# The last expert pair in four column groups, and two vectors on another DMA queue

## The chip, the cores and the metric

The kernel runs on one core of one Trainium2 chip. The metric is the device time of one execution in microseconds; each kernel is executed several times and the median counts. One execution per kernel is recorded by the hardware profiler, and the rows below come from that one. Five engines work side by side, each through its own list in order: TensorE (PE, matmuls; its weight loads are shown as PEld), VectorE (DVE), ScalarE (ACT), GpSimd (POOL) and SyncE (SP), which here mostly issues transfers. A "q" behind an engine's name (SPq, ACTq) is its queue of issued transfers.

## The reference, cut to what matters

One layer of an encoder on 512 tokens of 1024 columns. First a token mixer and a layer norm, then a mixture of experts and a second layer norm. The change touches only the end, the experts and the second norm:

```python
def expert_block(args):
    xs, e = args
    return (jax.nn.silu(xs @ w1[e]) * (xs @ w3[e])) @ w2[e]
...
y = yb.reshape(-1, d) * row_w[:, None].astype(x.dtype)
return jax.ops.segment_sum(y, rows, num_segments=t + 1)[:t]
...
moe = _hier_moe(x.reshape(-1, D_MODEL), ...)
x = _layer_norm(DEEPNORM_ALPHA * x + moe, ln2_g[layer], ln2_b[layer])
```

There are 32 experts with w1 and w3 of 1024 x 512 and w2 of 512 x 1024 in fp32, 2 MB each. Every token goes to two of them.

## The kernel before, in words

**Experts in pairs.** Experts are taken in 16 pairs `q` (0 to 15, `NP` is 16), 64 token places for each expert of a pair (`u` is 0 or 1). `gemm1` (line 1001) makes the first products with w1 (`m` = 0) and w3 (`m` = 1): the two experts of a pair use the two halves of PE's columns. `h` is their product after silu, `turn` (line 1016) transposes it to `hT`, and `gemm2` (line 1024) makes the second product with w2 into PSUM tiles `y`, one of 128 x 512 for columns 0 to 511 and one for 512 to 1023. `weigh` (line 1039) writes `y` times the token's weight as two addends of fewer bits: ACT writes `yh`, and DVE writes `yl`, the rest of `y` that `yh` leaves. `part` (line 1052) is the combine: PE multiplies the selection matrix `sel` with `yh` and `yl` of some columns, for a block `j` of 128 tokens, into a PSUM tile `cb`, and DVE adds that to the sum `xa`. For pairs 0 to 14 `combine` (line 1057) does this for the pair before, spread over the work of the present one.

**Weights.** `load_next` (line 664) issues the next of 96 loads on SP's queue, each of 2 MB, into nine slots of SBUF that are reused in turn. `queued` (line 115) keeps the transfers of one engine in the order of the program. A load waits until the products that read its slot's former content are done. The loads for w2 of the last pair are four halves of 1 MB (lines 686 to 691), the first two for columns 0 to 511, the others for the rest. When pair 14's w3 product is in the program, all 96 are issued.

**Order.** `kp` (line 98) pins an instruction behind the one before it in the program on the same engine, a transfer issued by an engine among them. An instruction on PE, DVE and ACT below runs in the order in which it is written, with one exception: the copy `onrow` (line 1165) is not pinned, and DVE's order starts anew there.

**Second norm's vectors.** At pair 14 (`q == NP - 2`, line 1110), behind `gemm1(q, 1)`, two transfers bring `ln2_g` and `ln2_b`, each copied to all 128 partitions (512 KB each), into `lnv`, the slot that this very product has read last. Before, they are issued on SP behind all weights. ACT's next instructions there in the program are the two copies of `xg` in `turn_rows` (line 905) and the copy of `hT`. At the end of pair 15 (lines 1120 to 1122) ACT copies `ln2_b` of one row to `off[0]` and DVE makes `off[1]`, the rest. `offset` (line 1169) multiplies them with a row of ones on PE, as the start of the last output's PSUM tiles `fp`.

**The last pair's second product.** It is cut by columns, `CS` (line 1143), in three groups: 512, 256 and 256. In program order: product and weighing of group 0; product and weighing of group 1; `add` of group 0 for all four token blocks; `squares` of the first 512 columns of blocks 0 and 1; `add` of group 1 for blocks 0 and 1; product and weighing of group 2; `squares` for blocks 2 and 3; `add` of group 1 for blocks 2 and 3; then for each block `add` of group 2 and `squares` of the second half. `add` (line 1148) is `part` on PE and, on DVE, the addition to `xa` that also sums the row into `sm2`; for group 0 a small DVE step `k2` follows. `squares` (line 1158) is on ACT and sums the squares of 512 columns around `k2`.

**The end.** From line 1225 on DVE makes means and variances, POOL a power, `newton` an iteration of it, ACT the diagonal matrices `dg`. The output of five of the eight tiles of 128 x 512 (`TURN`) goes through PE, with `dg` as weights (`scaled`), and ACT; DVE makes the other three (`finish`).

Of the kernel before, what the change touches and what calls it, by code (L numbers as in the profile page):

```python
# [10 lines left out]
F32 = mybir.dt.float32  # L11
# [6 lines left out]
ALU = mybir.AluOpType  # L18
# [4 lines left out]
D = 1024  # L23
K8 = 8
NT = 4
# [5 lines left out]
NP = NE // 2  # L31
# [38 lines left out]
def bcast_rows(ap2, n):  # L70

    return bass.AP(tensor=ap2.tensor, offset=ap2.offset, ap=[[0, 128], [1, n]])
# [7 lines left out]
def body(ctx, tc, nc, a):  # L80
    L, R = "left", "right"

    def pool(stack, name, side, **kw):
        return stack.enter_context(tc.tile_pool(name=name, bufs=1, side=side, reuse_waits="tile", **kw))
# [10 lines left out]
    def mm_tile(name="mm", tag="mm", shape=(128, 512)):  # L95
        return ps.tile(list(shape), F32, name=name, tag=tag, bufs=2 if tag == "lv" else 3)

    def kp(op):

        def pinned(*x, **y):  # L100
            ins = op(*x, **y)  # L101
            e = ins.ins.engine
            prev = next((i for i in reversed(nc.cur_bb.bb.instructions)
                         if i is not ins.ins and i.engine == e and type(i).__name__ != "BassTilePoolBoundary"), None)
            if prev is not None:
                edge(ins, prev.name)
            return ins
        return pinned

    def edge(ins, name):  # L110
        tc.add_manual_dep(ins.ins, name, mybir.DependencyInfo(mybir.DependencyClass.NoSync, mybir.DependencyReason.DATA), reason="order")
# [3 lines left out]
    def queued(op):  # L115

        def issue(*x, **y):
            ins = op(*x, **y)
            e = str(ins.ins.engine)
            if e in tail:  # L120
                edge(ins, tail[e])
            tail[e] = ins.ins.name
            return ins
        return issue
# [749 lines left out]
    def onehot_next(q):  # L874
        oq[q] = ep.tile([128, NT, 128], BF, name="oq", bufs=2)
        onehot(q, oq[q])
# [82 lines left out]
    ep = pool(ctx, "ep", R)  # L959
# [3 lines left out]
    j = NT - 1  # L963
# [21 lines left out]
    def first_fetch():  # L985

        yield
        p = slots(1, lambda j: ti[:, j, :], 2)
        tok1 = ep.tile([128, 1], F32, name="tok1")
        kp(nc.vector.tensor_reduce)(tok1, p[:, 0:2], axis=AX.X, op=ALU.add)  # L990
        pre["rows"] = fetch(tok1)
        run(share())
        yield
# [30 lines left out]
    def gemm2(q, st, cs=((0, 512), (512, 512)), last=True):  # L1024
        raw = [held[2, q, u] for u in range(2)]
        for c, d in cs:
            n, s = c // 512, slice(c % 512, c % 512 + d)
            if c % 512 == 0:
                st["y"][n] = mm_tile("y", "am")
            for f in range(4):  # L1030
                for u in range(2):
                    kp(nc.tensor.matmul)(st["y"][n][u * CAP:(u + 1) * CAP, s], st["hT"][:, f, u * CAP:(u + 1) * CAP],
                                         raw[u][:, f, c:c + d], start=(f == 0), stop=(f == 3))
        if last:
            for u in range(2):
                held.pop((2, q, u))
                load_next()

    def weigh(st, cs=((0, 512), (512, 512))):
        if "yh" not in st:  # L1040
            yy = mo.tile([128, 2, D], F32R, name="yy", tag="ln")
            st["yh"], st["yl"] = yy[:, 0], yy[:, 1]
            st["sel"] = ep.tile([128, T], F32R, name="sel")
            kp(nc.vector.tensor_scalar)(st["sel"], i512, -float(NOTOK), st["tw"][:, 0:1], op0=ALU.add, op1=ALU.is_equal)
        w = st["tw"][:, 1:2]
        for c, d in cs:
            s = slice(c, c + d)
            y = st["y"][c // 512][:, c % 512:c % 512 + d]
            kp(nc.scalar.activation)(st["yh"][:, s], y, AF.Copy, scale=w)
            kp(nc.vector.scalar_tensor_tensor)(st["yl"][:, s], y, w, st["yh"][:, s].bitcast(F32), op0=ALU.mult, op1=ALU.subtract)  # L1050
# [6 lines left out]
    def combine(st, first=False):  # L1057
        for i in range(8):
            j, c = divmod(i, 2)
            s = slice(c * 512, c * 512 + 512)  # L1060
            p = mm_tile("cb", ("mm", "am")[i % 2])
            part(p, st, j, c * 512, 512)
            if first:
                kp(nc.vector.scalar_tensor_tensor)(xa[:, j, s], xa[:, j, s], ALPHA, p, op0=ALU.mult, op1=ALU.add)
            else:
                kp(nc.vector.tensor_add)(xa[:, j, s], xa[:, j, s], p)
            yield
# [24 lines left out]
    for q in range(NP):  # L1092
        st = prs.setdefault(q, {"y": {}})
        old, last, back = prs.get(q - 1), q == NP - 1, iter(())
        if last:

            with tc.If(nov > 0):
                overflow(tc, nc, a, dram, x1d, xa, rc, ident, nblk, oh_, rk_, w_, nov, mm_tile, wp, *[slot[(len(order) - i) % len(HOME)] for i in (7, 8)])
            back = combine(old)
        p = gemm1(q, 0, first_fetch() if q == 0 else iter(()))  # L1100
        ac = wp.tile([128, FE], F32, name="ac", tag="btmp", bufs=2)
        kp(nc.scalar.activation)(ac, p, AF.Silu)
        if old and not last:
            gemm2(q - 1, old)
            weigh(old)
            back = combine(old, q == 1)
        if q > NP - 3:
            run(islice(back, 4 if last else 3))
        p = gemm1(q, 1)
        if q == NP - 2:  # L1110
            lnv = slot[(len(order) - 9) % len(HOME)].rearrange("p (i d) -> p i d", i=4)
            for i, x in enumerate((a["ln2_g"], a["ln2_b"])):
                queued(nc.sync.dma_start)(lnv[:, i], bcast_rows(x, D))
        h = wp.tile([128, FE], F32, name="h", tag="wraw", bufs=4)
        kp(nc.vector.tensor_mul)(h, ac, p)
        if last:
            run(islice(back, 3))
            st["hT"] = turn(h)
            run(back)
            off = [ep.tile([128, D], F32R, name="off", tag=t) for t in ("rows", "xg")]  # L1120
            kp(nc.scalar.copy)(off[0][0:1], lnv[0:1, 1])
            kp(nc.vector.tensor_sub)(off[1][0:1], lnv[0:1, 1], off[0][0:1].bitcast(F32))
            break
        xg = turn_rows(pre.pop("rows") if q == 0 else rows)
        for n in range(0 if q == 0 else q + 2, min(q + 3, NP)):
            prs.setdefault(n, {"y": {}})["tw"] = weights(n)
        if q < NP - 2:
            rows = fetch(prs[q + 2]["tw"][:, 0:1])
        if q < NP - 3:
            onehot_next(q + 3)  # L1130
        run(islice(back, 8 if q < NP - 2 else 3))
        st["hT"] = turn(h)
        run(back)
        if q == NP - 2:
            gemm2(q, st)
            weigh(st)
        if q == 1:
            run(cnt)
        if q == 3:
            nov = nc.values_load(novi[0:1, 0:1], min_val=0, max_val=NOV)  # L1140
        prs.pop(q - 1, None)

    CS = ((0, 512), (512, 256), (768, 256))
    sm2 = ep.tile([128, NT, 3], F32, name="n2s")
    sq2 = ep.tile([128, NT, 2], F32, name="n2q")
    k2, d2 = [ep.tile([128, NT], F32, name=n) for n in ("n2k", "n2d")]

    def add(j, i, tag):

        c, d = CS[i]  # L1150
        p = mm_tile("cb", tag)[:, 0:d]
        s = slice(c, c + d)
        part(p, st, j, c, d)
        kp(nc.vector.scalar_tensor_tensor)(xa[:, j, s], xa[:, j, s], 1.0, p, op0=ALU.mult, op1=ALU.add, accum_out=sm2[:, j, i:i + 1])
        if i == 0:
            kp(nc.vector.tensor_scalar)(k2[:, j:j + 1], sm2[:, j, 0:1], -1.0 / 512, None, op0=ALU.mult)

    def squares(j, n):

        junk = wp.tile([128, FE], F32, name="sq", tag="btmp", bufs=2)  # L1160
        kp(nc.scalar.activation)(junk, xa[:, j, hs[n]], AF.Square, bias=k2[:, j:j + 1], accum_out=sq2[:, j, n:n + 1])
# [10 lines left out]
        for i in range(2):  # L1172
            kp(nc.tensor.matmul)(pf[x], onrow, off[i][0:1, hs[x[1]]], start=(i == 0), stop=False)

    gemm2(NP - 1, st, [CS[0]], False)
    weigh(st, [CS[0]])
    gemm2(NP - 1, st, [CS[1]], False)
    weigh(st, [CS[1]])
    for j in range(NT):
        add(j, 0, ("mm", "lv")[j % 2])  # L1180
    squares(0, 0)
    squares(1, 0)
    add(0, 1, "mm")
    add(1, 1, "am")
    gemm2(NP - 1, st, [CS[2]])
    weigh(st, [CS[2]])
    squares(2, 0)
    squares(3, 0)
    add(2, 1, "lv")
    add(3, 1, "lv")  # L1190
    for j in range(NT):
        add(j, 2, ("mm", "lv")[j % 2])
        squares(j, 1)
    for i, x in enumerate(TURN):
        offset(x, "mm" if i < 3 else "am")
# [223 lines left out]
```

## Time and profile before

| | us |
|---|---|
| median of 3 runs | 1281.15 |
| lowest and highest | 1279.73 and 1282.1 |
| the profiled execution, its own time | 1280.67 |
| span of its records | 1278.0 |
| PE busy in the span | 1235.9 (97%) |
| DVE busy | 669.9 (52%) |
| ACT busy | 360.7 (28%) |
| mean rate of transfers | 224 GB/s |

Busy shares are means over a long row of stages with different limits: PE 97% doesn't say that PE limits the stage in question. Matmuls are pipelined and their ends are modelled, and some matmul records can be missing. The view of busy time by stretch tells for each stretch how busy each engine was, the granted clock of PE (1.00 is 2.4 GHz, 0.50 is 1.2 GHz), and the share of the 16 transfer engines in use. In the timeline a bracket tells how long the engine had been idle before a row and what released it; rows of the same kind that follow each other are merged (x and a count). A line number of 101 is that of `kp`, so most rows here have it; they are told apart by the tile names, out<-in.

### The profile page before, as it was taken

To read this page: it belongs to the slowest core of one execution; us is meant where nothing else is said; L and a number is where in the kernel's file an instruction comes from. 1 tells how busy PE (TensorE), PEld (TensorE's weight loads), DVE (VectorE), ACT (ScalarE), POOL (GpSimd) and SP (SyncE) were. 2 spreads that over 40 slices of the span, in tenths; PEclk is the share of its full clock that TensorE was granted. 3 is DMA by queue.
4 is the path that set the end of the run, shared out by engine and by line. 5 is a ranking of instruction groups with operands and counts; after the bars stand their busy time and mean duration, and the time that the engine had idled before them with its cause. 6 is when DMAs were issued, how large, how long until landed. Compare 5 with 4: busy or idle time off the path is not lost.

```text
span 1278.0 us, 20529 instructions
## 1 busy us (share of the span) xinstructions
PE 1235.9 (97%) x8369; PEld 851.2 (67%) x8369; DVE 669.9 (52%) x1412; ACT 360.7 (28%) x704; POOL 105.3 (8%) x117
## 2 busy tenths in 40 slices
PE   7999999999999999999999999999999999889997
PEld 7887877878778878888888798344444443333444
DVE  4587878877882246556555467332432222222326
ACT  4443444443452223222333231111111111111114
POOL 0031222302100000000000001100100000000000
PEclk9999999999999999999999999999999999999998
DMA  6322223222233333232335498999999999999992
GB/s 211 95 72 69 74 66 85 76 78 73 75 90 124 124 97 91 73 100 81 91 108 160 148 346 340 365 426 429 427 427 428 426 426 428 428 427 428 428 409 104
DMA packets 94000, 286.02 MB, mean 224 GB/s; under 512 B 13531, under 2 KB 71163, under 8 KB 81616
## 3 DMA queue, kind: packets, MB, share of 16 engines
q1 hardware_dynamic: 84112, 267.80, 54.6%
q10 hardware_dynamic: 7056, 10.78, 3.1%
q0 software_dynamic: 2736, 6.12, 1.2%
q8 instruction: 66, 1.08, 0.4%
q14 instruction: 30, 0.25, 0.1%
HBM read 282.19 MB, written 6.32 MB: 226 GB/s over the span
## 4 chain that ended last, share of the span: by engine, by line
PE 78%; DMA 15%; DVE 4%; ACT 1%; issue 1%; SPq 0%; POOL 0%; ACTq 0%; DVEq 0%; POOLq 0%
PE mm L237 13%; PE g L101 13%; DMA raw<-in_w_dram 12%; PE mm L239 12%; PE mm L238 12%; PE y L101 5%; PE op L101 3%; PE cb L101 3%; PE vp L252 2%; PE vp L253 1%; PE vp L254 1%; PE lv L386 1%; PE tr L101 1%; PE lv L421 1%; PE vp L101 1%; DMA raw<-in_ln_b_dram 1%
## 5 line engine op out<-in xcount | busy, mean ns | idle before, releaser
L101 PE MATMUL g<-raw,xg 128*64 128x512 f32 x1024 | 240.1, 602 | 15.4 <-DMA raw<-in_w_dram 15.0
L237 PE MATMUL mm<-xT,w 128*128 128x512 f32 x576 | 232.4, 403 | 1.1 <-ACT sg L276 0.7
L239 PE MATMUL mm<-xT,w 128*128 128x512 f32 x576 | 226.4, 393 | 0.0
L238 PE MATMUL mm<-xT,w 128*128 128x512 f32 x576 | 225.4, 391 | 0.0
L101 PEld LDWEIGHTS g<-raw,xg 128*64 128x64 f32 x1024 | 76.8, 138 | 161.5 <-issue 133.2
L161 DVE TENSOR_TENSOR w<-wraw,w 128x512 fp32r<-128x512 f32 x216 | 141.4, 690 | 45.7 <-ACT w L160 45.6
L160 ACT CAST w<-wraw 128x512 fp32r<-128x512 f32 x216 | 121.1, 621 | 110.4 <-PE mm L239 99.6
L237 PEld LDWEIGHTS mm<-xT,w 128*128 128x128 f32 x576 | 108.9, 189 | 24.0 <-ACT sg L276 1.1
L239 PEld LDWEIGHTS mm<-xT,w 128*128 128x128 f32 x576 | 108.8, 189 | 23.4
L238 PEld LDWEIGHTS mm<-xT,w 128*128 128x128 f32 x576 | 109.0, 189 | 20.9
L101 PE MATMUL y<-raw,hT 128*64 128x512 f32 (+1 forms) x528 | 116.3, 580 | 0.3 <-ACT hT L101 0.3
L101 DVE SCALAR_TENSOR_TENSOR yy<-y,tw,yy 128x512 fp32r<-128x512 f32 (+1 forms) x33 | 24.1, 734 | 174.1 <-ACT yy L101 171.0
L101 PEld LDWEIGHTS y<-raw,hT 128*64 128x64 f32 x528 | 41.6, 137 | 71.2 <-issue 64.8
L101 DVE TENSOR_TENSOR xa<-xa,cb 128x512 f32<-128x512 f32 x112 | 68.6, 682 | 9.0 <-PE cb L101 8.6
L101 DVE TENSOR_TENSOR h<-ac,g 128x512 f32<-128x512 f32 x16 | 11.0, 688 | 114.3 <-PE g L101 114.3
L276 ACT ACTIVATE sg<-mm 128x512 f32<-128x512 f32 x56 | 33.5, 598 | 121.6 <-PE mm L239 115.4
L101 PE MATMUL cb<-yy,sel 128*128 128x512 f32 (+1 forms) x264 | 66.4, 397 | 1.1 <-DVE yy L101 0.8
L252 PE MATMUL vp<-w,xT 128*128 128x256 f32 x224 | 65.2, 291 | 0.0
L254 PE MATMUL vp<-w,xT 128*128 128x256 f32 x224 | 63.4, 283 | 0.0
L253 PE MATMUL vp<-w,xT 128*128 128x256 f32 x224 | 63.3, 282 | 0.0
L101 PEld LDWEIGHTS cb<-yy,sel 128*128 128x128 f32 x264 | 47.2, 188 | 15.1 <-issue 2.4
L101 ACT COPY xg<-tr 128x512 f32<-128x512 f32 x31 | 16.7, 589 | 130.8 <-PE tr L101 130.8
(302 smaller groups left out, 1662.1 us busy)
## 6 DMA issues: line engine op xcount, KB each, us to landing
raw<-in_w_dram SPq DMA_DIRECT2D x92, 2048.0 KB, 30.4
wraw<-in_w_in_dram SPq DMA_DIRECT2D x176, 256.0 KB, 3.2
raw<-in_w_dram SPq DMA_DIRECT2D x8, 1024.0 KB, 9.2
wraw<-in_w_branch_hg_dram SPq DMA_DIRECT2D x16, 256.0 KB, 3.2
wraw<-in_w_branch_ret_dram SPq DMA_DIRECT2D x16, 256.0 KB, 3.4
wraw<-in_w_out_dram SPq DMA_DIRECT2D x16, 256.0 KB, 3.5
rs<-rd ACTq DMA_DIRECT2D x12, 256.0 KB, 4.2
xr<-in_x_dram SPq DMA_DIRECT2D x4, 512.0 KB, 7.3
```

What stands on the lines that cost most here:

```text
L101: ins = op(*x, **y)
L160: nc.scalar.copy(hi[:, s, :], raw)
L161: nc.vector.tensor_sub(lo[:, s, :], raw, hi[:, s, :].bitcast(F32))
L237: nc.tensor.matmul(p, w[0][:, k, sl], rhs(0, k), start=(k == 0), stop=False)
L238: nc.tensor.matmul(p, w[0][:, k, sl], rhs(1, k), start=False, stop=False)
L239: nc.tensor.matmul(p, w[1][:, k, sl], rhs(0, k), start=False, stop=(k == K8 - 1))
L252: op(nc.tensor.matmul)(o, x2[0][:, k, ts], w[0][:, k, :], start=(k == 0), stop=False)
L253: op(nc.tensor.matmul)(o, x2[1][:, k, ts], w[0][:, k, :], start=False, stop=False)
L254: op(nc.tensor.matmul)(o, x2[0][:, k, ts], w[1][:, k, :], start=False, stop=(k == K8 - 1))
L276: nc.scalar.activation(s, p, AF.Sigmoid)
L386: nc.tensor.matmul(p[b:b + WB, j, 0:WB], lhs[:, j * 128 + b:j * 128 + b + WB], rhs(j * 128 + b), start=True, stop=True)
L421: nc.tensor.matmul(p8[:, i, :], C[:, j * 128:j * 128 + 128], QQ[:, 1 - b, (1 - b) * 256:(1 - b) * 256 + 256], start=True, stop=True)
```

## The change

Two edits. The transfers of `ln2_g` and `ln2_b` are issued by ACT in its pinned order, and no longer by SP behind the weights. And the last pair's second product, its weighing and its additions are cut in four groups of 256 columns. The new order in the program: product and weighing of group 0; product and weighing of group 1, `add` of group 0 for four blocks; product and weighing of group 2, then for each block `add` of group 1 and `squares` of the first half; product and weighing of group 3, `add` of group 2 for four blocks; then for each block `add` of group 3 and `squares` of the second half. Groups 0 and 1 share one PSUM tile of `y`, groups 2 and 3 the other. `k2` comes from 256 columns in place of 512.

```diff
@@ -1110,7 +1110,7 @@
         if q == NP - 2:
             lnv = slot[(len(order) - 9) % len(HOME)].rearrange("p (i d) -> p i d", i=4)
             for i, x in enumerate((a["ln2_g"], a["ln2_b"])):
-                queued(nc.sync.dma_start)(lnv[:, i], bcast_rows(x, D))
+                kp(nc.scalar.dma_start)(lnv[:, i], bcast_rows(x, D))
         h = wp.tile([128, FE], F32, name="h", tag="wraw", bufs=4)
         kp(nc.vector.tensor_mul)(h, ac, p)
         if last:
@@ -1140,8 +1140,8 @@
-    CS = ((0, 512), (512, 256), (768, 256))
-    sm2 = ep.tile([128, NT, 3], F32, name="n2s")
+    CS = tuple((256 * i, 256) for i in range(4))
+    sm2 = ep.tile([128, NT, 4], F32, name="n2s")
     sq2 = ep.tile([128, NT, 2], F32, name="n2q")
@@ -1153,7 +1153,7 @@
         if i == 0:
-            kp(nc.vector.tensor_scalar)(k2[:, j:j + 1], sm2[:, j, 0:1], -1.0 / 512, None, op0=ALU.mult)
+            kp(nc.vector.tensor_scalar)(k2[:, j:j + 1], sm2[:, j, 0:1], -1.0 / 256, None, op0=ALU.mult)
@@ -1172,24 +1172,16 @@
-    gemm2(NP - 1, st, [CS[0]], False)
-    weigh(st, [CS[0]])
-    gemm2(NP - 1, st, [CS[1]], False)
-    weigh(st, [CS[1]])
+    for i in range(4):
+        gemm2(NP - 1, st, [CS[i]], i == 3)
+        weigh(st, [CS[i]])
+        if i:
+            for j in range(NT):
+                add(j, i - 1, ("mm", "lv")[j % 2])
+                if i == 2:
+                    squares(j, 0)
     for j in range(NT):
-        add(j, 0, ("mm", "lv")[j % 2])
-    squares(0, 0)
-    squares(1, 0)
-    add(0, 1, "mm")
-    add(1, 1, "am")
-    gemm2(NP - 1, st, [CS[2]])
-    weigh(st, [CS[2]])
-    squares(2, 0)
-    squares(3, 0)
-    add(2, 1, "lv")
-    add(3, 1, "lv")
-    for j in range(NT):
-        add(j, 2, ("mm", "lv")[j % 2])
+        add(j, 3, ("mm", "lv")[j % 2])
         squares(j, 1)
     for i, x in enumerate(TURN):
         offset(x, "mm" if i < 3 else "am")
```

## Rows read from the trace of the kernel before

**Rows 1.** Busy time by stretch of the last 128 us: start and end, length, then busy time and count of PE, PEld, DVE, ACT and POOL, PE's granted clock, the share of the transfer engines and GB/s.
```profile
1150.00:1200.00 50.00, 46.74 (x223) 20.58 (x221) 15.09 (x31) 5.67 (x10) 3.89 (x4) 1.00 1.01 427
...
1250.00:1260.00 10.00, 9.47 (x61) 5.40 (x57) 6.13 (x20) 4.30 (x9) 0.00 (x0) 1.00 0.01 5
```

**Rows 2.** The chain of work that ended last, in order of time, from 1199 us to its end: start, us, and what it was.
```profile
1199.57 29.44 DMA raw<-in_w_dram
...
1238.28 2.55 SPq L118
...
1240.88 11.01 DMA raw<-in_ln_b_dram
...
1253.22 1.21 DVE off L101
...
1262.49 0.18 DVE n2m L101
...
1273.32 0.58 ACT raw L101
```

**Rows 3.** The timeline of PE and PEld from 1229 to 1265 us: start, us, engine, line, operation, tiles, shapes, count, and the idle time before it with what released it.
```profile
1229.06 0.20 PEld L101 LDWEIGHTS g<-raw,xg 128*64 128x64 f32 x4 [1.17 <-DMA raw<-in_w_dram]
...
1238.93 0.23 PEld L101 LDWEIGHTS g<-raw,xg 128*64 128x64 f32 x4 [0.63 <-DMA raw<-in_w_dram]
...
1248.80 5.38 PE L101 MATMUL y<-raw,hT 128*64 128x512 f32 x32 [0.26 <-ACT hT L101]
...
1257.43 1.95 PE L101 MATMUL y<-raw,hT 128*64 128x256 f32 x16
...
1259.31 2.47 PE L101 MATMUL cb<-yy,sel 128*128 128x256 f32 x12
...
1260.47 1.10 PEld L101 LDWEIGHTS cb<-yy,sel 128*128 128x128 f32 x7 [0.33 <-DVE yy L101]
...
1261.70 2.70 PE L101 MATMUL fp<-off,onrow 1*128 1x512 f32 x10
```

**Rows 4.** Transfers issued between 1190 us and the end: tiles, queue, count, KB each, median us from issue to landing.
```profile
raw<-in_w_dram SPq DMA_DIRECT2D x3, 2048.0 KB, 29.4
...
raw<-in_ln_g_dram SPq DMA_DIRECT2D x1, 512.0 KB, 12.4
raw<-in_ln_b_dram SPq DMA_DIRECT2D x1, 512.0 KB, 11.0
rows<-x1d,ix POOLq DMA_INDIRECT x1, 10.4
```

**Rows 5.** The timeline of ACT and DVE from 1252 to 1263 us, columns as in rows 3.
```profile
1252.14 1.04 ACT L101 CAST off<-raw 1x1024 fp32r<-1x1024 f32 x1 [3.39 <-DMA raw<-in_ln_b_dram]
...
1254.36 1.12 DVE L101 SCALAR_TENSOR_TENSOR yy<-y,tw,yy 128x512 fp32r<-128x512 f32 x2
...
1256.48 0.68 DVE L101 SCALAR_TENSOR_TENSOR xa<-xa,cb 128x512 f32<-128x512 f32 x1
...
1257.27 0.68 DVE L101 SCALAR_TENSOR_TENSOR xa<-xa,cb 128x512 f32<-128x512 f32 x1
...
1259.43 0.47 ACT L101 ACTIVATE yy<-y,tw 128x256 fp32r<-128x256 f32 x1 [1.16 <-PE y L101]
...
1259.93 0.48 DVE L101 SCALAR_TENSOR_TENSOR yy<-y,tw,yy 128x256 fp32r<-128x256 f32 x1 [0.31 <-ACT yy L101]
1260.33 0.41 DVE L101 SCALAR_TENSOR_TENSOR xa<-xa,cb 128x256 f32<-128x256 f32 x1
...
1261.01 0.42 DVE L101 SCALAR_TENSOR_TENSOR xa<-xa,cb 128x256 f32<-128x256 f32 x1
...
1261.35 0.42 DVE L101 SCALAR_TENSOR_TENSOR xa<-xa,cb 128x256 f32<-128x256 f32 x1
1261.53 0.72 ACT L101 ACTIVATE sq<-xa,n2k 128x512 f32<-128x512 f32 x1 [0.23 <-DVE xa L101]
...
1262.25 0.71 ACT L101 ACTIVATE sq<-xa,n2k 128x512 f32<-128x512 f32 x1
```

**Rows 6.** The timeline of PE, ACT and SP from 1215 to 1221 us, with one of ACT's output transfers of the end, columns as in rows 3. The time of an SPq or ACTq row is what the issue took the engine.
```profile
1216.54 1.16 PE L101 MATMUL tr<-cf,rows 128*128 128x128 f32 x8
...
1216.72 16.20 SPq L118 DMA_DIRECT2D raw<-in_w_dram  x1
...
1217.34 1.07 ACT L101 COPY xg<-tr 128x512 f32<-128x512 f32 x2 [9.74 <-PE tr L101]
...
1220.45 1.08 PE L101 MATMUL y<-raw,hT 128*64 128x512 f32 x4
...
1268.79 0.34 ACTq L101 DMA_DIRECT2D out_dram<-raw  x1
```

**Rows 7.** Busy time by stretch around the statistics and the scaling, columns as in rows 1, and below them weight loads of PE's scaling matmuls and DVE's last step from the timeline.
```profile
1264.00:1265.00 1.00, 0.41 (x2) 0.00 (x0) 0.39 (x1) 0.46 (x2) 0.98 (x1) 0.52 0.00 0
...
1270.00:1271.00 1.00, 1.00 (x2) 0.34 (x1) 1.00 (x2) 0.46 (x1) 0.00 (x0) 0.57 0.68 262
...
1271.54 0.19 PEld L101 LDWEIGHTS fp<-raw,dg 128*128 128x128 f32 x1 [0.24 <-issue]
...
1271.97 0.19 PEld L101 LDWEIGHTS fp<-raw,dg 128*128 128x128 f32 x1 [0.24 <-issue]
...
1272.57 0.75 DVE L101 SCALAR_TENSOR_TENSOR raw<-raw,n2y 128x512 f32<-128x512 f32 x1
```

## The prediction, made before the changed kernel ran

> **What bounds the kernel now.** I read the busy time by stretch first. Up to about 1248 us the transfers are full: the DMA share is 1.01 at 427 GB/s, and TensorE (PE), though nearly always busy, is not the limit [rows 1]. Where the two meet is seen in PE's own order of time: both gate products of the last expert pair stop for weights, 1.17 us until 1229.06 and 0.63 us until 1238.93 [rows 3]. The chain of waits says the same: a transfer ending at 1229.01, then PE, then the transfer of ln_b, DVE's off, and at last the means and the output [rows 2]. Behind the last weights the transfers are empty (share 0.01 from 1250 to 1260) and PE, ACT and DVE take turns [rows 1].
>
> So two places count. Until 1238.93 each byte put ahead of a weight load costs its transfer time. From the start of the last second product, T = 1248.80 [rows 3], the order among PE, ACT and DVE counts, up to DVE's first step on the means at 1262.49, T + 13.69 [rows 2]. From there to the end of the span are 15.5 us of statistics, scaling and output, which the change hardly touches.
>
> **Part 1: the vectors through ACT's queue.** Removed: two DMAs at the end of SP's queue. They were issued at 1238.28 and 1240.88 [rows 2], since SP was held up by its own full queue (one issue before them took 16.20 us, [rows 6]), and landed 12.4 and 11.0 us later [rows 4], at 1250.68 and 1251.89, behind all weights. Added: the same two on ACT, pinned behind pair 13's weighing. They wait only for their slot, free when the product before PE's transposes at 1216.54 ends [rows 6]. Queued behind them on ACT are the two xg copies at 1217.34 [rows 6] and the hT copy behind them. An issue on ACT takes 0.34 us [rows 6], so the copies move by some 0.7 us; the hT copy leads to pair 14's second product, which ends before the PE's wait of 1.17 us for weights, so that wait hides it (without it: up to 0.7 us).
>
> What matters is where 1 MB goes. Landing 1.21 us apart, each 512 KB took 1.21 us, so both are 2.42 us of all transfer engines; 1.05 MB at 427 GB/s [rows 1] gives 2.46. In the kernel before they ran behind the last weights, beside PE's work. On ACT's queue at 1217 they meet a backlog: weights of SP's queue take 29.4 us to land, but a gather issued on POOL's queue lands in 10.4 [rows 4]; a second queue is not served behind the first. The vectors land long before 1238.93, and each weight then still outstanding lands about 2.45 us later. PE's second wait moves to 1241.4. Its work ahead cannot absorb that, it waits there already. T becomes 1251.25. Price: +2.45, between 0 (served behind the backlog) and 2.46.
>
> The Trainium skill, "DMA: Bandwidth & Descriptors", section "Issuing engines are not separate DMA queues", speaks against this part too: queues of different engines run on the same 16 DMA engines and interleave, and a second one saves only issue time. By it the vectors displace weights, as the gather's landing suggests; the sum would be the same +2.45.
>
> Gained: ACT's off copy waited 3.39 us for ln_b [rows 5] and stood ahead of the first weighing, as DVE's off (1.21) did for the second half of it [rows 2]. In the new order off runs from about T to T + 1.0 on ACT and to 2.25 on DVE, while PE makes the first product. The gain is inside the next sum.
>
> **Part 2: four column groups.** The numbers of products and additions by area stay; the additions go from twelve to sixteen, and PE's combine matmuls with 256 columns from 16 to 32. Durations: a 256-column second product keeps PE 1.88 us (1257.43 to the next work at 1259.31) and ACT starts on it 2.00 after its start; DVE's yl starts 0.50 after ACT's yh (1259.43, 1259.93) and keeps DVE 0.40; PE resumes 0.54 after yl began; a combine matmul is (1261.70 - 1260.47)/7 = 0.176, eight are 1.39 [rows 3, 5]. An addition is 0.34 from start to start, and its ACT square starts 0.52 after it, squares 0.71 apart [rows 5]. Those with the k2 step were 0.79 at 512 columns [rows 5]; 0.52 at 256 is my estimate, 0.27 less.
>
> Counted from T, in program order on each engine. Product 0 starts at 0, yh0 at 2.00, yl0 at 2.50. Product 1 writes the other half of the same PSUM tile; no row shows whether PE has to wait for the readers of the first half. The ends are 0 and 1.29 (PE free at 1.75, yl0 read at 3.04). Before, the second product into such a tile, at 1257.43, came 2 us behind the last read of the first [rows 3, 5], and so shows neither. I take the wait, since the program orders accesses to a tile and the halves share one. Then product 1 runs 3.04 to 4.92, yh1 at 5.04, yl1 at 5.54. Combine 0 on PE 4.92 to 6.31, its additions on DVE 5.94 to 8.02. Product 2 6.31 to 8.19, yh2 8.31, yl2 8.81 to 9.21. Combine 1 8.19 to 9.58, additions from 9.21 to 10.57. Product 3 9.58 to 11.46.
>
> Here a new wait arises. ACT has the four squares of the first half ahead of yh3, pinned in program order. They follow the additions: 9.73, 10.44, 11.15, 11.86, and ACT is free at 12.57, though product 3 was readable at 11.58. Behind yh3 stands yl3 (13.07), and behind yl3 on DVE stand the four additions of group 2, whose products PE finished long before. DVE is idle from 10.57 to 13.07, 2.5 us; before, its largest such gap was 0.31 [rows 5]. Then the additions of group 2 run 13.47 to 14.83 and those of group 3 to 16.2, beside combine 3 (from 13.6). The means start at T + 16.3 in place of 13.69: +2.6. Without the wait in the tile all up to yh3 comes 1.4 earlier: T + 14.9, +1.2.
>
> The Trainium skill, "PSUM — Partial Sum Buffer", section "PSUM bank collisions raise a hardware error", says that two engines may not touch one bank and quadrant at once, even in different columns. By it the tile wait is needed, and its branch of the sum, +2.6, holds; no row of before shows it.
>
> **Sum.** 2.45 + 2.6 = 5.05. The profiled execution took 1280.67 (span 1278.0 and 2.67 around it); it would take 1285.7. The median, 1281.15, is 0.48 above the profiled one: 1286.2.
>
> The last part has its own uncertainty. PE's granted clock, 2.4 GHz up to there, fell to 1.2 at about 1264, behind the one-row off matmuls that end there, and came back shortly before 1271, amid the scaling products; a scaling matmul passes in 0.43 us at the higher level (1271.54 to 1271.97), twice that at half the clock [rows 7]. If in the new run all of them lie in the low stretch, the last four cost up to 1.7 more; if none does, DVE's last step, at 1272.57 to 1273.32 [rows 7], against ACT's last copy to 1273.90 [rows 2], caps the gain at 0.6.
>
> **Rivals.** (a) The forecast, 1286.2, 52%, within -0.6 and +1.7. (b) No wait inside the PSUM tile: 2.45 + 1.2, 1284.8, 17%. (c) The other side, no slower than the bound below: the vectors cost nothing. Their packets would have to stay behind the backlog until the gate weights that landed at 1238.93 are through; later they displace only halves of the last second product's weights, of which the second half is not needed until T + 6. Then part 2 remains: 1283.7, and 1282.4 without the tile wait. For it: SP's backlog is 29 us deep; against it: the gather's 10.4 us in the same backlog [rows 4]. 14%. (d) ACT reaches yh3 in time. The finer groups do start DVE 3.06 us earlier (yl0 at 2.50 against 1254.36 - 1248.80 = 5.56, [rows 3, 5]). If the squares don't hold yh3 up, PE alone decides: with no tile wait product 3 is readable at 10.15, yh3 and yl3 take 0.9 up to 11.05, and the eight additions behind them 2.72 and 0.1 at the end: T + 13.9, +0.2. With the vectors' price that is 1283.8, with (c) 1281.4. It decides where ACT is free before 10.2; against it: four squares of 0.71 from 8.3 on even without the tile wait. 9%. (e) ACT is blocked in issuing as SP was: 16.2 us from 1216.7, the xg and hT copies late to about 1234 and pair 14's second product with them (it began at 1220.45 by [rows 6]); 14 less the two weight waits (1.8) and plus part 2 is some 15 us, 1296. For it: SP's 16.20; against it: that was SP's own queue, and ACT's is empty. 4%. (f) The clock's bad case on the forecast, 1288, 4%.
>
> **How the numbers follow.** Likeliest is (a), 1286.2. The range goes from 1283.0, under (b) and most of (c), to 1288.3, the forecast with its dearer clock and a little; outside are (e), a part of (c), and (d) where it meets (c). About 0.2%, 2.56 us, is what a measurement here can tell from none: 1278.6 to 1283.7 counts as the same. Slower: (a), (b), (e), (f), and what clock and rounding lift of (c) and (d) over that line, 82%. The same: the rest of (c) and (d), 15%. Faster: no sum of mine reaches it, 3% for what I can't see.
>
> **What would show it.** Right: PE's two weight waits end at some 1231.4 and 1241.4, and the vectors land before 1241; the second product starts near 1251.2; PE pauses 1.3 us behind the first group's 16 matmuls until DVE's yl; DVE pauses some 2.5 us before the last yl, with ACT on squares; the means come near 1267.5. Wrong: weight waits at the old times (c), no PE pause behind group 0 (b), ACT's last yh directly behind its product (d), ACT busy issuing (e).

## The result, and the profile after

The changed kernel takes 1287.70 us (median of 5 runs, 1286.99 to 1288.36) against 1281.15 before (5 runs, 1279.73 to 1282.27): a ratio of 1.0052, 95% interval 1.0041 to 1.0063. It is slower by 6.55; the forecast was slower by 5.05, at 1286.2 within 1283.0 to 1288.3.

The profiled execution took 1288.18, its span is 1286.3, 8.3 longer than before. I cut both spans at three events: A, the start of pair 14's w3 product on PE, ahead of everything that the change moves; T, the start of the last second product; and the first step on the means. The row of A, from PE's timeline of the kernel before and then of the one after:

```profile
1209.33 7.27 PE L101 MATMUL g<-raw,xg 128*64 128x512 f32 x32
```

```profile
1211.95 7.26 PE L101 MATMUL g<-raw,xg 128*64 128x512 f32 x32
```

So 2.62 of the 8.3 lie ahead of A, where both kernels run the same code. They are not the change: kernel e3 below, with the same code up there, has its A at 1211.81 and is no slower than the kernel before, and in the other kernels below A lies anywhere between 1208.80 and 1212.39. All that follows is therefore measured from A and from T. A serves for these two kernels, where it lies 29.80 and 29.81 behind W, the end of the weight wait in pair 13's w3 product (1179.53 before, 1182.14 after). For some of the kernels below it does not, and W takes its place.

| | before | after | forecast of the difference | measured |
|---|---|---|---|---|
| A to the end of the first weight wait | 19.73 | 22.19 | +2.45 | +2.46 |
| A to T | 39.47 | 42.82 | +2.45 | +3.35 |
| T to the means | 13.69 | 15.99 | +2.6 | +2.30 |
| means to the end of the span | 15.51 | 15.54 | 0 | +0.03 |
| sum from A | | | +5.05 | +5.68 |

PE and PEld after, from 1229 to 1258 us, the rows that answer to [rows 3] (columns as there):

```profile
1234.13 0.20 PEld L101 LDWEIGHTS g<-raw,xg 128*64 128x64 f32 x4 [3.66 <-DMA raw<-in_w_dram]
...
1244.88 0.20 PEld L101 LDWEIGHTS g<-raw,xg 128*64 128x64 f32 x4 [0.36 <-issue]
...
1254.77 1.95 PE L101 MATMUL y<-raw,hT 128*64 128x256 f32 x16 [0.26 <-ACT hT L101]
...
1257.82 1.95 PE L101 MATMUL y<-raw,hT 128*64 128x256 f32 x16 [1.09 <-DVE yy L101]
```

The first weight wait grew from 1.17 to 3.66. The second is gone, since PE arrives late: the bracket names no transfer any more. The last row is the wait in the PSUM tile, 1.09 for DVE's read of the first half. The chain of waits after (start, us, what), in the stretch of [rows 2]:

```profile
1202.43 31.67 DMA raw<-in_w_dram
...
1234.14 8.78 PE g L101 x30
...
1254.77 1.97 PE y L101 x16
...
1257.28 0.50 DVE yy L101
...
1257.82 1.95 PE y L101 x16
1259.76 1.14 PE cb L101 x8
1260.90 1.90 PE y L101 x16
...
1265.52 1.60 ACT sq L101 x5
1267.12 0.37 ACT yy L101
1267.51 0.48 DVE yy L101
1268.00 2.74 DVE xa L101 x16
1270.76 0.18 DVE n2m L101
```

ln_b and `off` have left the chain. In their place stand the tile wait (PE y, DVE yy, PE y) and, at the end, ACT's squares ahead of the last weighing. ACT and DVE after (columns as in [rows 5]):

```profile
1214.10 0.34 ACTq L101 DMA_DIRECT2D raw<-in_ln_g_dram  x1
1215.82 0.33 ACTq L101 DMA_DIRECT2D raw<-in_ln_b_dram  x1
...
1254.62 1.04 ACT L101 CAST off<-raw 1x1024 fp32r<-1x1024 f32 x1
...
1266.32 0.71 ACT L101 ACTIVATE sq<-xa,n2k 128x512 f32<-128x512 f32 x1
1267.03 0.45 ACT L101 ACTIVATE yy<-y,tw 128x256 fp32r<-128x256 f32 x1
1267.51 0.48 DVE L101 SCALAR_TENSOR_TENSOR yy<-y,tw,yy 128x256 fp32r<-128x256 f32 x1 [2.33 <-ACT yy L101]
```

`off` starts at T - 0.15, as wanted; DVE stands still for 2.33 before the last yl, because ACT's square stands directly ahead of the last yh.

### The profile page after: what moved, and what is told of

It is laid out like the page before. It is cut to its first block, busy times and chain, and to the rows that moved or that the text cites. A ratio compares the mean times of both kernels' runs of the same rounds, so it can differ in the third digit from the quotient of the medians.

```text
span 1286.3 us, 20589 instructions
## 1 busy us (share of the span) xinstructions
PE 1240.8 (96%) x8393; PEld 855.3 (66%) x8393; DVE 670.6 (52%) x1421; ACT 361.0 (28%) x705; POOL 102.2 (8%) x117
## 4 chain that ended last, share of the span: by engine, by line
PE 75%; DMA 17%; DVE 6%; ACT 1%; issue 1%; POOL 0%; ACTq 0%; SPq 0%; DVEq 0%; POOLq 0%
DMA raw<-in_w_dram 14%; PE g L101 12%; PE mm L237 12%; PE mm L239 12%; PE mm L238 12%; PE y L101 5%; PE op L101 3%; PE cb L101 3%; DMA rs<-rd 2%; PE vp L252 1%; DVE w L161 1%; PE vp L253 1%; PE vp L254 1%; PE lv L421 1%; PE vp L101 1%
```

## The experiments

The theory at first was the forecast's: the vectors' megabyte displaces weights, and in the tail the PSUM tile and ACT's order each cost over 1 us. The rivals: one edit costs nothing, or the tail would gain if it were only set right. Kernels e1, e2, e3 and e5 shared a chip, e6, e8, e9 and e10 a second, the last three a third; the kernel before took 1281.27, 1281.56 and 1280.68 there.

For comparing all kernels A is no fixed point. In e1, e5, e8 and e9 the product behind W took 8.42 to 8.62 us, at the lower clock, and in the others 7.08. So PE reached A 30.71 to 30.91 behind W in those four, and 29.80 or 29.81 behind it in the others. The transfers did not move with PE: in the five kernels with no megabyte ahead of the gate weights, e9 among them, the first weight wait ends 49.52 or 49.53 behind W. The product behind W in the kernel before, and then in e9:

```profile
1179.53 7.08 PE L101 MATMUL g<-raw,xg 128*64 128x512 f32 x30 [2.71 <-DMA raw<-in_w_dram]
```

```profile
1180.01 8.50 PE L101 MATMUL g<-raw,xg 128*64 128x512 f32 x30 [2.72 <-DMA raw<-in_w_dram]
```

So the table counts from W; T is given from A too, as the expectations name it. What the kernels gave:

| kernel | W | first weight wait ends, from W | second | T from W | T from A | means from T | us | ratio, 95% |
|---|---|---|---|---|---|---|---|---|
| before | 1179.53 | 49.53 | 59.40 | 69.27 | 39.47 | 13.69 | 1281.15 | |
| after | 1182.14 | 51.99 | none | 72.63 | 42.82 | 15.99 | 1287.70 | 1.0052, 1.0041 to 1.0063 |
| e1_queue_only | 1181.18 | 52.01 | 63.75 | 73.63 | 42.81 | 12.91 | 1284.72 | 1.0026, 1.0017 to 1.0036 |
| e2_groups_only | 1180.33 | 49.53 | 59.34 | 69.22 | 39.42 | 20.71 | 1287.98 | 1.0058, 1.0045 to 1.0072 |
| e3_one_row | 1182.00 | 49.52 | 59.42 | 69.30 | 39.49 | 12.90 | 1279.97 | 0.9989, 0.998 to 0.9998 |
| e5_own_tiles | 1181.23 | 52.01 | 63.40 | 73.29 | 42.58 | 14.67 | 1285.98 | 1.0037, 1.0023 to 1.0051 |
| e6_squares_behind | 1179.82 | 51.97 | 61.82 | 71.70 | 41.89 | 14.85 | 1285.33 | 1.0035, 1.0021 to 1.0049 |
| e8_pool_queue | 1181.48 | 51.96 | 61.82 | 71.70 | 40.79 | 15.99 | 1286.08 | 1.0043, 1.003 to 1.0057 |
| e9_four_free | 1180.01 | 49.52 | 59.41 | 69.29 | 38.49 | 13.52 | 1280.69 | 0.9996, 0.9987 to 1.0006 |
| e10_between | 1180.83 | 49.53 | 59.38 | 69.27 | 39.47 | 12.90 | 1280.36 | 0.9992, 0.9983 to 1.0002 |
| e11_pool_three | 1180.49 | 52.03 | none | 72.44 | 42.63 | 12.91 | 1282.77 | 1.0014, 1.0005 to 1.0023 |
| e12_pool_double | 1180.16 | 52.89 | none | 74.55 | 44.74 | 12.90 | 1284.91 | 1.003, 1.0018 to 1.0042 |
| after_again | 1179.00 | 52.00 | 63.07 | 72.96 | 43.16 | 15.98 | 1285.19 | 1.0037, 1.0023 to 1.005 |

**e1, the queue alone** (the kernel before, with one line changed):

```diff
-                queued(nc.sync.dma_start)(lnv[:, i], bcast_rows(x, D))
+                kp(nc.scalar.dma_start)(lnv[:, i], bcast_rows(x, D))
```

> Part 1 alone: the vectors on ACT's queue, the three column groups of before. By the forecast's mechanism the last weight waits end 2.45 us later; with the half-clock stretch that the changed kernel showed behind its longer wait (8.78 instead of 7.08 us for the first gate product, +1.7) and the second wait gone (-0.8) the second product starts 3.3 later, and in the tail the early off lets the first yl start at T + 4.4 instead of 5.56, so -1.1: 1283.4 us, +2.2. Rival, the vectors cost nothing in the queue and the whole loss is in the groups: -1.1, 1280.0.

It is slower by 3.45 where 2.2 was expected, and the rival, a gain, is out. The tail gained 0.78 by the early `off`; T, counted from W, moved by 4.36, not 2.45. PE's timeline of e1:

```profile
1233.19 7.08 PE L101 MATMUL g<-raw,xg 128*64 128x512 f32 x30 [1.96 <-DMA raw<-in_w_dram]
...
1244.93 0.20 PEld L101 LDWEIGHTS g<-raw,xg 128*64 128x64 f32 x4 [2.48 <-DMA raw<-in_w_dram]
```

The product between the two waits takes 7.08, against 8.78 in the changed kernel, and the second weights come 4.35 later than before; PE waits 2.48 for them. That T from A is the same in both kernels is chance: from W e1 is 1.00 later, and the two lose their time behind the first wait in different ways.

**e2, the groups alone** (the changed kernel, with e1's line put back to SP).

> Part 2 alone: four groups, the vectors on SP behind the weights as before. The start T of the second product stays as before, with weight waits of about 1.2 and 0.6 us. ACT's off waits for ln_b to T + 3.1 again, so the first yh comes at T + 4.3, the first yl at 5.6 behind DVE's off, and product 1, which waits for that yl in the shared tile, at 6.1 instead of 3.05: the means at T + 19.1 (16.0 + 3.06), +5.4 us, 1286.5. Rival, four groups are harmless and the loss is the queue's: 1281.

It is as slow as the whole change, with T where it was before. ACT's `off` waits 3.46 for ln_b, and the first group's weighing stands behind it on both engines. PE of e2:

```profile
1249.55 1.95 PE L101 MATMUL y<-raw,hT 128*64 128x256 f32 x16 [0.26 <-ACT hT L101]
...
1255.69 3.58 PE L101 MATMUL y<-raw,hT 128*64 128x256 f32 x16 [4.20 <-DVE yy L101]
```

The tile wait is 4.20 here, and behind it the same 16 matmuls take 3.58 in place of 1.95: the granted clock is 0.50 from 1256 to 1258. That the means came at T + 20.71, 1.6 later than expected, is this product. So the two edits are no sum of two prices: the groups need the early vectors.

**e3, one row for `off`** (the kernel before; only the 4 KB row that `off` reads is fetched early, into a free part of the slot):

```diff
+            b2 = lnv[0:1, 2]
+            kp(nc.scalar.dma_start)(b2, a["ln2_b"])
...
-            kp(nc.scalar.copy)(off[0][0:1], lnv[0:1, 1])
-            kp(nc.vector.tensor_sub)(off[1][0:1], lnv[0:1, 1], off[0][0:1].bitcast(F32))
+            kp(nc.scalar.copy)(off[0][0:1], b2)
+            kp(nc.vector.tensor_sub)(off[1][0:1], b2, off[0][0:1].bitcast(F32))
```

> The kernel before with one addition: a single row of ln2_b (4 KB) is loaded early through ACT's queue for off alone; the two broadcasts stay on SP behind the weights. If the gain of the change lies in off no longer waiting and the loss in the megabyte and the groups, T stays, the first yl starts at T + 4.4 instead of 5.56, and the means come 1.1 us earlier: 1280.0. Rival, DVE's chain behind it has slack that swallows the earlier start: 1281.1.

T stays (69.30 from W for 69.27), the means come 0.79 earlier, the time is 1.30 lower: the interval lies just below 1. All that the early vectors are worth in the tail is bought by this row, without the megabyte.

**e5, a PSUM tile for each group** (the changed kernel; in `gemm2` and `weigh`):

```diff
+            if d == 256:
+                n, s = c, slice(0, d)
-            if c % 512 == 0:
+            if c % 512 == 0 or d == 256:
                 st["y"][n] = mm_tile("y", "am")
...
-            y = st["y"][c // 512][:, c % 512:c % 512 + d]
+            y = st["y"][c][:, 0:d] if d == 256 else st["y"][c // 512][:, c % 512:c % 512 + d]
```

> The changed kernel with each of the four products in a PSUM tile of its own, so that product 1 need not wait for the readers of product 0. If the wait of 1.09 us in the shared tile is what delays it, product 1 follows product 0 at once and the means come 1.1 to 1.4 us earlier: 1286.5. Rival, ACT's squares and DVE's order set the end whatever PE does: 1287.7.

The means come at T + 14.67, 1.32 earlier than in the changed kernel. The pause on PE is gone; the first two products run as one row of 32:

```profile
1254.52 3.67 PE L101 MATMUL y<-raw,hT 128*64 128x256 f32 x32 [0.26 <-ACT hT L101]
```

**e6, the first squares behind the last weighing** (the changed kernel):

```diff
         weigh(st, [CS[i]])
+        if i == 3:
+            for j in range(NT):
+                squares(j, 0)
         if i:
             for j in range(NT):
                 add(j, i - 1, ("mm", "lv")[j % 2])
-                if i == 2:
-                    squares(j, 0)
```

> The changed kernel with the four squares of the first half moved behind the last weighing in ACT's order; nothing else. In the changed kernel product 3 was readable at 1265.83 and ACT's last yh started at 1267.03, behind the squares. If that is what holds DVE's additions up, the means come 1.2 us earlier: 1286.5. Rival, PE's combine of group 3 or DVE's own work sets the end: 1287.7.

The means come at T + 14.85, 1.14 earlier, and ACT's last yh now waits for PE's product and for nothing else (T is 1251.52, so it runs at T + 11.10). ACT of e6:

```profile
1262.62 0.48 ACT L101 ACTIVATE yy<-y,tw 128x256 fp32r<-128x256 f32 x1 [2.57 <-PE y L101]
```

**e8, the vectors on POOL's queue** (the changed kernel, with `nc.gpsimd` for `nc.scalar` in e1's line). It asks why the second weights came 4.35 and 4.00 us late in e1 and e5. In the changed kernel SP issued a weight at 1202.43 and the next at 1231.78, 49.64 after W; before, it had resumed at 1214.48, 34.95 after W. SP's waits between 1200 and 1233 us after (who waited and where, for whom: us, times, longest):

```profile
SPq L1097 <- SPq L1097: 28.8, 6, 7.4
```

Line 1097 is the branch `tc.If(nov > 0)` ahead of the last pair; before, SP stood there for 14.2. It resumed 0.15 after ln_b landed (1215.82 plus 15.8). The theory: SP waits in the branch for the transfers of ACT's queue too, and while it waits it issues no weights.

> The changed kernel with the two vectors issued on POOL's queue at the same place, not on ACT's. The trace of the changed kernel showed more than a megabyte's displacement: SP, at its branch ahead of the last pair, waited until the second vector had landed (1231.6), issued the next weights only at 1231.78, and the transfer engines fell to 0.39 of their share from 1230 to 1232. SP's branch waits for completions of the SP and ACT queues, not for POOL's. If that wait is part of the price, SP resumes some 7 us behind the start of pair 14's w3 product, the rate has no dip, the second gate weights are there 32.0 us behind that start instead of 32.9, and the time is 0.9 us less: 1286.8. Rival, the displaced megabyte alone costs all of 3.3 us: 1287.7.

Busy time by stretch (columns as in [rows 1]) of the changed kernel, and then of e8:

```profile
1230.00:1232.00 2.00, 1.17 (x4) 0.19 (x2) 0.75 (x1) 0.69 (x1) 0.00 (x0) 1.00 0.39 160
1232.00:1234.00 2.00, 0.00 (x0) 0.00 (x0) 0.00 (x0) 0.00 (x0) 0.00 (x0) 1.00 0.73 147
1234.00:1236.00 2.00, 1.86 (x6) 0.67 (x8) 0.00 (x0) 0.00 (x0) 0.00 (x0) 0.66 0.98 410
1236.00:1238.00 2.00, 2.00 (x6) 0.49 (x4) 0.00 (x0) 0.00 (x0) 0.00 (x0) 0.50 0.95 410
```

```profile
1230.00:1232.00 2.00, 1.44 (x4) 0.19 (x2) 0.75 (x1) 0.69 (x1) 0.00 (x0) 1.00 0.99 416
1232.00:1234.00 2.00, 0.56 (x4) 0.27 (x6) 0.00 (x0) 0.00 (x0) 0.00 (x0) 1.00 1.02 426
```

With ACT's queue the transfers run dry (share 0.39, then 0.73); with POOL's they stay full. SP of e8 resumes 34.95 after W, as before, although ln_b, issued later than 1214.65, took 16.3 to land:

```profile
1216.43 1.52 SPq L118 DMA_DIRECT2D raw<-in_w_dram  x3
```

That part of the theory is shown, and the other traces agree. In the five kernels with the vectors on ACT's queue SP resumed about 0.15 behind ln_b's landing, 48.39 (e6) to 50.74 (e1) after W. Even the one 4 KB row on ACT's queue moved it, to 40.31 in e3 and 41.17 in e9, at no cost to T.

What the hold is worth hangs on when it ends. In e6 it ended at 48.39, and the second weights came at 61.82, just as in e8 without it. In e1 and e5 it ended at 50.74 and 50.63, and they came at 63.75 and 63.40, 1.9 and 1.6 later. PE's second wait in e6, and then three pieces of the chain of waits of e1, which runs through SP's first issue behind the branch:

```profile
1241.64 0.27 PEld L101 LDWEIGHTS g<-raw,xg 128*64 128x64 f32 x4 [0.59 <-DMA raw<-in_w_dram]
```

```profile
1231.92 0.34 SPq L118
...
1232.37 12.52 DMA raw<-in_w_dram
...
1244.93 7.08 PE g L101 x30
```

e8's T is 0.93 earlier than the changed kernel's, but there the clock differs too (7.08 for 8.78), and the intervals of the two ratios overlap.

**e9, four groups with no wait left** (e5's and e6's edits and e3's row, with the two vectors on SP as before).

> Four groups without the waits found: each product in a PSUM tile of its own, squares behind the last weighing, the broadcasts on SP behind the weights as before, and a single row of ln2_b loaded early for off. Start of the second product as before (39.5 us behind the start of pair 14's w3 product). By the order counted from T, product 3 is readable at 10.15, the last yl starts at 10.65, and eight additions follow it: the means at T + 13.9, 1281.3, as the kernel before and 1.0 us behind the same early off with three groups. Rival, the finer groups gain once nothing holds them up: T + 12.9 or less, 1280.0.

T + 13.52, between theory and rival. It is 0.17 better than the three groups of the kernel before, and 0.62 worse than the three groups of e3, which also have `off` early. Even freed of both waits, four groups lose to three in the tail; the intervals of the two ratios overlap.

**e10, the megabyte ahead of the last halves** (the kernel before; in `load_next`, behind the halves of the last w2 for columns 0 to 511, and the old place removed):

```diff
+                        if c == 0:
+                            lnv = slot[(len(order) - 9) % len(HOME)].rearrange("p (i d) -> p i d", i=4)
+                            for i, x in enumerate((a["ln2_g"], a["ln2_b"])):
+                                queued(nc.sync.dma_start)(lnv[:, i], bcast_rows(x, D))
```

> The kernel before with one edit: the two broadcasts stay on SP's queue but go between the halves of the last w2 loads, behind columns 0 to 511 and ahead of the rest. No weight is late that PE waits for: the first halves land as before, the second ones 2.4 us later, at about 1252, when the second group's product begins; the vectors land about 1247.7, ahead of off. So the start of the second product stays and the tail gains what the early off gains: 1280.0. Rival, a megabyte ahead of any weights costs its 2.45 us: 1282.6.

The same megabyte, ahead of 2 MB of weights, costs nothing: T at 69.27 from W, as before, and the early `off` is gained. It displaces only what PE doesn't wait for.

**e11, the queue alone, on POOL, and e12, the megabyte twice.** e11 is e1 with `nc.gpsimd`. e12 loads the same vectors a second time into a free part of the slot; the copy is not used:

```diff
                 kp(nc.gpsimd.dma_start)(lnv[:, i], bcast_rows(x, D))
+                kp(nc.gpsimd.dma_start)(lnv[:, 2 + i], bcast_rows(x, D))
```

> The three column groups of before, the two vectors on POOL's queue. With no wait of SP's branch for the vectors, only the displaced megabyte is left: the second gate weights about 2.4 us later than before, the second product 41.9 us behind the start of pair 14's w3 product (39.5 before, 42.8 with the vectors on ACT's queue), the means at T + 12.9: +1.6, 1283.0. Rival, SP's wait costs nothing net, and the time is as with ACT's queue: T at 42.8, 1284.7.

> The same with two more transfers of 512 KB, the two vectors once more into a free part of the slot: 2 MB ahead of the last weights. If the price of the queue is the displaced bytes, the second product is a further 2.4 us later, 44.3 behind the start of pair 14's w3 product, and the time 1285.4. Rival, bytes are absorbed as long as SP isn't held up: as with one pair of vectors, 1283.0.

The second megabyte adds 2.11 to T and 2.14 to the time, where its transfer alone would take some 2.4. But 2.11 is no measure of the transfer: PE's first wait ends only 0.86 later, and the rest is the product behind it, 9.79 in place of 8.55. What the bytes do displace is the last weights: the first half of w2 whose landing is on record, issued at the same distance from W, took 33.1 us to land in place of 30.6.

e11's T is 1.19 earlier than e1's on ACT's queue, though from A, at 42.63, it looks no earlier; its loss against the kernel before is 2.09, e1's 3.45, with intervals that overlap. It is 0.74 later than e8's, with the product at 8.55 in place of 7.08. PE of e11, and then of e12, shows the product behind the weight wait:

```profile
1232.52 8.55 PE L101 MATMUL g<-raw,xg 128*64 128x512 f32 x30 [2.81 <-DMA raw<-in_w_dram]
```

```profile
1233.06 9.79 PE L101 MATMUL g<-raw,xg 128*64 128x512 f32 x30 [3.66 <-DMA raw<-in_w_dram]
```

**after_again**, the changed kernel once more, beside e11 and e12.

> The changed kernel itself, beside the two others on the same chip: 1287.7, the second product 42.8 us behind the start of pair 14's w3 product, the means at T + 16.0. If the single profile of it was a chance case, these two differ by over 1 us.

Its stretches come again: 52.00 from W to the first weights, T at 72.96 for 72.63, means at T + 15.98. Its time is 4.51 above the kernel before, not 6.55. From W its profile adds up to +3.69 +2.29 -0.55 = +5.4, so the 2 us between the two ratios are not in the stretches that the change touches.

## Why the prediction was right, and where its sizes were off

**The vectors' price: mechanism right, term mis-sized.** The term "Price: +2.45" was 3.35 at T. The first weight wait did end 2.46 later, and 2.43 to 2.50 later in all seven kernels with the vectors once ahead of the gate weights, so the transfers displace weights by their own length. The Trainium skill, "DMA: Bandwidth & Descriptors", section "Issuing engines are not separate DMA queues", says that transfers of all issuing engines share the same 16 DMA engines; the 2.43 to 2.50, on ACT's queue and on POOL's alike, agree. Rival (c), free vectors, is out by e1 (+3.45). e10 shows the condition under which it would have held: issued behind the gate weights, the megabyte costs 0.00 at T.

What the step "PE's second wait moves to 1241.4" left out is two things behind the first wait. One: in the changed kernel PE's granted clock fell from 2.4 to 1.2 GHz while its weight loads waited 3.66 (1.00, 0.66, 0.50 in the stretches above), so the first gate product took 8.78 in place of e1's 7.08, PE reached the second product only 62.75 after W, and the second wait vanished under it. Two: where the clock stayed up, in e1 and e5, the second weights came 4.35 and 4.00 late, since SP was held in its branch until the vectors had landed.

The cases without either loss are e6 and e8, with the product at 7.08 and the second weights at 61.82: T moved by 2.43 in both, the forecast's number. Over the seven kernels with the vectors ahead of the gate weights once, the price at T, from W, was +2.43 (e6, e8) to +4.36 (e1). What goes beyond 2.43 is the clock in e11 (+3.17, POOL's queue, no hold) and in the changed kernel (+3.36, where PE no longer waited), and SP's hold in e1 and e5 (+4.36, +4.02). In after_again (+3.69) both occur, and the hold ended last: PE came late by a product of 8.48 and still waited 0.42. With no megabyte ahead of them T lay 69.22 to 69.30 behind W in five kernels, so the differences are no scatter.

**The moment of issue was wrong, without effect.** "They wait only for their slot, free when the product before PE's transposes at 1216.54 ends": ACT issued them at 1214.10 and 1215.82, while that product ran (1211.95 to 1219.2). The two issues lie 1.72 apart, near a quarter of that product, so the slot seems to come free by parts as the product reads them. The rest of the step held: the issues took 0.34 and 0.33, they landed after 10.1 and 15.8 us, and the xg copies came right behind PE's transposes. Rival (e), ACT blocked in issuing, is out.

**The tail: +2.30 for +2.6.** Both waits are there, and each is worth about what was said: own tiles give back 1.32 (the prediction has 1.4, and 1.29 by its own "PE free at 1.75, yl0 read at 3.04"), squares behind the weighing 1.14 (1.2 expected of e6). The steps ahead came nearly to the hundredth: product 1 at T + 3.05 (forecast 3.04), yl1 at 5.55 (5.54). Most of the 0.3 comes in at the term "eight are 1.39" (eight times its 0.176 would be 1.41): the first group's eight combine matmuls passed in 1.14 (chain above), so yh2 came at 8.06 for 8.31, and all behind it moved with it, the last yh to 12.26 for 12.57, the last yl to 12.74 for 13.07. Rival (b), no wait in the tile, is out by the 1.09 on PE and by e5. The Trainium skill, "PSUM — Partial Sum Buffer", section "PSUM bank collisions raise a hardware error", says that two engines may not touch one bank and quadrant at once, so such a wait is needed; the trace shows the wait, and no run here shows that hardware would need it: two engines in one bank with no wait between them were not tried. Rival (d), ACT in time, is e6 with e5: e9 has both, and came to 13.52 where (d) had 13.9.

**The end** stayed: 15.54 for 15.51. The clock's bad case, (f), did not occur there.

**The sum.** +5.68 from A by the first profile, +5.4 by the second, +5.05 forecast. The median's 6.55 holds about 1 more that no stretch of the change accounts for, and after_again's 4.51 about 1 less; what lies ahead of A and around the span changes from run to run by that much. Which of the two is nearer to the truth is open; both intervals lie above 1.002. That 1287.70 lies inside the range, 0.6 under its top, is in part luck: the top stood for a dearer clock among the scaling products, and what came was a lower clock at the gate weights and that scatter.

**The better version** is e3: the kernel before with one 4 KB row fetched early, 1279.97 against 1281.27, ratio 0.9989 (0.998 to 0.9998), a gain of about 0.1%.

## What to carry to other kernels

A transfer that changes its queue still takes its bytes from the same engines: place it by what is waited for behind it, after the last bytes that hold up the compute engine, and fetch early only what is read early (here 4 KB of 1 MB). In this tail finer groups could pay only if each group's writer and reader did not meet in one tile and if nothing in program order stood ahead of the next group's first reader; even then the added steps cost more than the earlier start brought (e9 against e3). When two edits are made together, run each alone: here the groups alone cost as much as both, because the early vectors hid a wait that the groups would have laid bare. And when kernels are compared stretch by stretch, start from an event of what limits there: where the transfers limited, PE's own event A wandered by 1.1 us between kernels with the same code ahead of it.

## What was not expected of the hardware

PE's granted clock fell to half after a wait for weights in the middle of a busy stretch, and the product behind it ran 1.4 to 2.7 us longer: 8.78, 8.48, 8.55 and 9.79 in after, after_again, e11 and e12, whose first weight loads had waited 3.63 to 4.54. In e1, e5 and e8, with 2.70 to 2.95, it took 7.08, and in e6 too, with 3.63. At W, where weight loads waited 3.58 to 3.60 in eight kernels, the product took 7.08 in four of them (before, e3, e6, e10) and 8.42 to 8.62 in the other four. So a wait can cost more than its own length, and the same wait not in each run.

A transfer on ACT's queue held up the issues on SP's: SP stood in a branch until the vectors had landed, and the shared transfer engines fell to a share of 0.39 in a stretch that the kernel needs them for. On POOL's queue the same transfers did not hold it. The hold cost nothing where it ended 48.39 after W, and 1.6 to 1.9 us where it ended at 50.63 and 50.74.
